# Hybrid decoder step on one core: the sample tokens' outer products as one fp32r matmul over 96 stacked rows, and their state products in four column groups

## The chip, the core and the metric

One Trainium2 chip (trn2), one of its cores. The metric is the device time of one execution in microseconds (us), the median of the runs shown; less is better. The core's engines are TensorE (PE; its weight loads are listed apart as PEld), VectorE (DVE), ScalarE (ACT), GpSimd (POOL) and SyncE (SP), which here only issues DMAs.

## The reference

One layer of a decoder for a prompt of 2048 tokens and, beside it, a batch of 8 sequences with 4 new tokens each (the 32 "sample" rows). Each token passes an HGRN2 recurrence and a sliding-window attention, which gates merge, and then an MLP with a squared ReLU. What the change touches is the recurrence of the sample rows, with four heads of 128 x 128 state for each of the 8 sequences:

```python
def step(S, inp):                       # one chunk; here the chunk is the 4 new tokens
    qc, lc, kc, vc = inp
    b = jnp.cumsum(lc, axis=-2)
    o_inter = jnp.einsum('bhcd,bhde->bhce', qc * jnp.exp(b), S)
    ...
    o_intra = jnp.einsum('bhts,bhse->bhte', attn, vc)
    bl = b[..., -1:, :]
    S_new = jnp.exp(bl[..., 0, :])[..., None] * S + jnp.einsum('bhsd,bhse->bhde', kc * jnp.exp(bl - b), vc)
    return S_new, o_inter + o_intra
```

`o_inter` is called the state products below, the second term of `S_new` the outer products. All arithmetic is float32.

## The kernel before

The prompt is worked in four blocks of 512 tokens, b0 to b3. The 32 sample rows (NS = 32) ride with block b3. Weights and activations of the large products are split into a high and a low part of type fp32r, and each product is three matmuls (high times high, high times low, low times high), lines 165 to 167, 264 to 266 and 1580 to 1582. The recurrence's own matmuls have float32 operands; such a matmul stands as two records in the trace, with two weight loads.

A scheduler sets the order on each engine when the kernel is built: the program text gives the dependences, and independent work of neighbouring stages is interleaved. Each engine then runs its list in that order and waits on semaphores. Buffers come from rings ("tags"); the next user of a ring's buffer waits until the last reader of it is done.

The part of block b3 that matters here, in order:

* Attention of the last prompt chunk: `pc_b3c` (masked probabilities, ring t4), `po_b3c` (values, line 1108), `ob_b` (its split, line 258).
* The recurrence's levels (`hgrn_levels`): at each of seven levels (two for the sample rows) DVE scales `W_b` (lines 776, 777), PE forms small blocks `lv_b3g` (prompt) and `lv_b3s` (sample) with line 771, four 32-row blocks of one PSUM bank side by side, and DVE copies them out under a mask (line 788). Matmuls of the gate columns, `ps_hgb`, are put between as filler.
* The chunk loop: `o_b3o`, `u_b3o`, `state`, one tail (`on_b3o`, transposes `oT_b3o`, line 1174) per chunk, with `ybb` matmuls (lines 165 to 167; `pb_b`, line 1258, takes their results on DVE) as filler.
* The sample part, lines 1209 to 1238, from 1387.7 us of the profile on. For each head h: SP loads the state `S0_h` (512 KB, shown as `S`, line 1221); PE multiplies `aS` by `vS` (one matmul, 32 rows, line 1222) and, for each of the 8 sequences b, a 128 x 32 column block of `qb` with `S0_h`'s block b (line 1224). All nine add up in the same 32 rows of PSUM, `o_smp`. `qb` holds a sequence's 4 query columns and zeros elsewhere, so the nine can share the rows. DVE spreads `vS` into `vb` (32 x 1024, row s only in its own sequence's block, line 1226) and scales `S0_h` (line 1230). Two matmuls `kn_smp` by `vb` (32 rows, 512 columns each, line 1233, `us`) give the outer products, DVE adds each to its half of `S0_h` (line 1234), and SP writes the state out (`out_new_s_sample`, line 1235).
* The sample tail: `hgrn_out` takes four sums of squares from `o_smp` on ACT (line 205), a power on POOL (line 200), and scales into `on_smp` on DVE (line 1164); `hgrn_tail` transposes it (`oT_smp`, line 1172). Then come the splits into `oa_b` and the `yab` matmuls.

`S0_h` and `vb_h` share the ring t4 of three buffers, so a load of the next state waits until the matmuls that read an older `vb` are done, and a `vb` may wait until a state has been written out. `kn_smp`, the `on_` tiles and others share the ring t2, also of three. SP issues state loads, state writes and weight loads (`r_ubb`, `r_uab`, line 138) in one list, so a waiting load holds up those behind it.

## Time and profile before

| | |
|---|---|
| median of 3 runs | 2823.07 us (2819.94 to 2825.53) |
| profiled execution | span 2810.0 us from the first to the last instruction; the 13.1 us to the median lie around it |
| PE busy | 2730.1 us (97% of the span) |
| DVE busy | 1791.2 us (64%) |
| ACT busy | 1110.0 us (40%) |
| POOL busy | 490.9 us (17%) |
| mean granted TensorE clock | 0.993 |

Times inside the program are counted from the span's start. A row of the timeline gives start, length, engine, line, operation, output and inputs, shape and count; in brackets stands the idle time of the engine before it and what ended that, where "issue" means that the profile shows nothing the engine waited for. The records of successive matmuls overlap, so what a matmul costs PE is read from start to start. Of a PE form such as 128*32 128x16, the first part is the weight block (contraction rows by columns) and the second the moving operand.

### The profile page before, as it was taken

Reading aid. Unit: us, or ns where it says so; the run is one execution under the profiler, and the core shown is the slowest. Engines: PE = TensorE matmul, PEld = TensorE weight load, DVE = VectorE, ACT = ScalarE, POOL = GpSimd, SP = SyncE. Lnnn points to the kernel's source line nnn. Section 1 sums busy time; section 2 is a strip of 40 time slices with the busy share of each in tenths; the row PEclk is TensorE's granted clock in tenths of the full one; section 3 lists DMA queues with packets and bytes.
Section 4 is the critical chain, followed back from the end, with each engine's and each line's share of the span. In section 5 each row is a group of like instructions: output and inputs, shape, how many; then the busy total and the mean of one; then the engine's idle time right before and its main releaser. Section 6 shows DMA issues by size and latency. Waiting matters only on the chain.

```text
span 2810.0 us, 50089 instructions
## 1 busy us (share of the span) xinstructions
PE 2730.1 (97%) x20053; PEld 2403.9 (86%) x20053; DVE 1791.2 (64%) x2905; ACT 1110.0 (40%) x2070; POOL 490.9 (17%) x782
## 2 busy tenths in 40 slices
PE   8999999999999999899999999999999999999998
PEld 7778888788899977677898888878888999999998
DVE  5675746746774385637667777765567777654556
ACT  4542445423344353335334333434344233343332
POOL 1100211002300102320231221220012343320001
PEclk9999999999999999999999999999999999999999
DMA  5237662377743424652365544796566444485553
GB/s 190 75 103 237 208 198 76 97 242 256 251 126 115 144 76 149 219 160 67 105 210 184 181 145 150 265 317 222 190 200 215 147 161 135 155 291 184 189 187 119
DMA packets 344481, 487.60 MB, mean 174 GB/s; under 512 B 23432, under 2 KB 220824, under 8 KB 344248
## 3 DMA queue, kind: packets, MB, share of 16 engines
q1 hardware_dynamic: 289112, 329.10, 37.5%
q0 software_dynamic: 42880, 140.22, 13.8%
q10 hardware_dynamic: 12256, 15.08, 1.5%
q8 instruction: 157, 2.57, 0.4%
q14 instruction: 76, 0.62, 0.1%
HBM read 353.64 MB, written 130.68 MB: 172 GB/s over the span
## 4 chain that ended last, share of the span: by engine, by line
PE 78%; DMA 6%; DVE 6%; issue 5%; ACT 2%; POOL 2%; SPq 0%; POOLq 0%; DVEq 0%; ACTq 0%
PE f L1581 6%; PE f L1582 6%; PE f L1580 6%; PE fB_f L264 4%; PE fB_f L266 3%; PE fB_f L265 3%; PE fD_f L264 2%; PE fD_f L266 2%; PE fD_f L265 2%; PE ps_hfb L684 2%; PE fB_z L264 1%; PE fB_z L266 1%; PE fB_z L265 1%; PE wob L1390 1%; PE gab L166 1%
## 5 line engine op out<-in xcount | busy, mean ns | idle before, releaser
L1582 PE MATMUL f<-f2S,lw2T 128*128 128x264 f32 (+1 forms) x576 | 184.4, 320 | 2.0 <-DVE lw2T L152 2.0
L1580 PE MATMUL f<-f2S,hw2T 128*128 128x264 f32 (+1 forms) x576 | 184.5, 320 | 1.6 <-ACT hw2T L151 1.6
L1581 PE MATMUL f<-f2S,hw2T 128*128 128x264 f32 (+1 forms) x576 | 184.0, 319 | 0.0
L264 PE MATMUL fB_f<-S,w1T_f 128*128 128x264 f32 (+1 forms) x384 | 123.2, 322 | 3.1 <-ACT c_f L327 2.2
L152 DVE TENSOR_TENSOR lw2T<-lw2T,hw2T 128x1024 fp32r<-128x1024 f32 x64 | 78.2, 1224 | 69.7 <-ACT hw2T L151 68.8
L265 PE MATMUL fB_f<-S,w1T_f 128*128 128x264 f32 (+1 forms) x384 | 122.5, 319 | 0.0
L1580 PE MATMUL f<-f2A,h_w2B 128*128 128x264 f32 (+1 forms) x384 | 122.4, 319 | 0.0
L1581 PE MATMUL f<-f2A,h_w2B 128*128 128x264 f32 (+1 forms) x384 | 122.3, 319 | 0.0
L1582 PE MATMUL f<-f2A,l_w2B 128*128 128x264 f32 (+1 forms) x384 | 122.3, 318 | 0.0
L266 PE MATMUL fB_f<-S,w1T_f 128*128 128x264 f32 (+1 forms) x384 | 122.0, 320 | 0.0
L151 ACT CAST hw2T<-lw2T 128x1024 fp32r<-128x1024 f32 x64 | 67.2, 1051 | 137.2 <-DMA lw2T<-w_T 137.2
L1582 PEld LDWEIGHTS f<-f2S,lw2T 128*128 128x128 f32 x576 | 108.4, 188 | 10.4 <-DVE lw2T L152 2.9
L1580 PEld LDWEIGHTS f<-f2S,hw2T 128*128 128x128 f32 x576 | 108.8, 189 | 9.9 <-ACT hw2T L151 2.4
L1388 PE MATMUL wob<-m_b,h_wob 128*128 128x512 f32 (+2 forms) x320 | 113.1, 353 | 3.2 <-ACT h_wob L257 3.2
L1390 PE MATMUL wob<-m_b,l_wob 128*128 128x512 f32 (+2 forms) x320 | 112.4, 353 | 3.0 <-DVE l_wob L258 2.8
L1581 PEld LDWEIGHTS f<-f2S,hw2T 128*128 128x128 f32 x576 | 108.8, 189 | 7.6
L1389 PE MATMUL wob<-m_b,h_wob 128*128 128x512 f32 (+2 forms) x320 | 112.5, 352 | 0.0
L152 DVE TENSOR_TENSOR f2S<-f2S 128x1024 fp32r<-128x1024 f32 (+1 forms) x64 | 78.9, 1240 | 41.3 <-ACT f2S L151 40.9
L257 ACT CAST w1T_f<-w1r_f 128x512 fp32r<-128x512 f32 x128 | 77.1, 619 | 69.7 <-DVE w1r_f L300 29.7
L258 DVE TENSOR_TENSOR w1T_f<-w1r_f,w1T_f 128x512 fp32r<-128x512 f32 x128 | 87.4, 688 | 26.0 <-ACT w1T_f L257 25.7
L1507 POOL DMA_DIRECT2D u_A<-c_f x106 | 57.4, 541 | 236.1 <-DVE c_f L1491 225.1
L1507 POOL DMA_DIRECT2D u_S<-s_f x144 | 77.7, 541 | 109.0 <-DVE s_f L1502 92.4
(845 smaller groups left out, 9256.8 us busy)
## 6 DMA issues: line engine op xcount, KB each, us to landing
w1r_f<-w_ff SPq DMA_DIRECT2D x64, 512.0 KB
lw2T<-w_T SPq DMA_DIRECT2D x64, 512.0 KB
rw2B<-w_ff SPq DMA_DIRECT2D x48, 512.0 KB
f2S<-u_S SPq DMA_DIRECT2D x32, 528.0 KB
ws<-w_ff SPq DMA_DIRECT2D x32, 512.0 KB
r_wob<-w_o SPq DMA_DIRECT2D x32, 512.0 KB
f2S<-u_S SPq DMA_DIRECT2D x32, 512.0 KB
u_S<-s_f POOLq DMA_DIRECT2D x96, 132.0 KB, 2.3
```

What stands on the lines that cost most here:

```text
L152: pin(nc.vector.tensor_tensor(lo, F(lo), F(hi), ALU.subtract), on)
L258: pin(nc.vector.tensor_tensor(dl, src, F(dh), ALU.subtract), on)
L264: nc.tensor.matmul(ps, wh, ah, start=(first and k == 0), stop=False, skip_group_check=not first)
L265: nc.tensor.matmul(ps, wh, al, start=False, stop=False, skip_group_check=not first)
L266: nc.tensor.matmul(ps, wl, ah, start=False, stop=(last and k == 3), skip_group_check=not first)
L1388: nc.tensor.matmul(p, wh, ah, start=(k == 0), stop=False)
L1389: nc.tensor.matmul(p, wh, al, start=False, stop=False)
L1390: nc.tensor.matmul(p, wl, ah, start=False, stop=(k == KD - 1))
L1507: nc.gpsimd.dma_start(us[o][u.n // 4][u.n % 4 * P:(u.n % 4 + 1) * P, u.t0:u.t0 + u.ln], y_)
L1580: nc.tensor.matmul(ps, wh, ah, start=first, stop=False, skip_group_check=cont)
L1581: nc.tensor.matmul(ps, wh, al, start=False, stop=False, skip_group_check=cont)
L1582: nc.tensor.matmul(ps, wl, ah, start=False, stop=lastk, skip_group_check=cont)
```

## The change

Four things change in the sample part.

1. The outer products. `kn3` holds 96 rows: the high part (fp32r) of the keys, their low part, and the high part again; `v3` holds high, high and low part of `vS`. One fp32r matmul over the 96 rows then gives the three products of a split pair. `vb` is spread from `v3`, 96 x 1024, and the mask `m_b` gets 96 rows. New instructions, once for all heads: four casts of 32 x 512 on ACT (one of them takes the place of the copy of `kn_smp`), two subtractions of 32 x 512 on DVE.
2. The state products. Sequence b's matmul writes the rows 32 (b mod 4) onward, so that four 32-row groups of the PSUM bank collect two sequences each. The `aS` by `vS` matmul comes last and adds to group 0.
3. At the end the four groups are added: one copy of 32 x 512 on ACT and three additions of 32 x 512 on DVE into `os`, and `hgrn_out` reads `os` instead of `o_smp`.
4. `kn3` and `v3` lie in the ring t2 and stay there over all heads.

```diff
-            kn = k_natural(kS, 0, NS, "smp")
+            kn3, v3 = (wk.tile([P, 512], F32R, tag="t2", bufs=3, name=n) for n in ("kn3", "v3"))
+            kps = k_turn(kS, 0, NS, "smp")
+            nc.scalar.copy(kn3[0:NS], kps[0:NS])
+            tt(kn3[NS:2 * NS], kps[0:NS], F(kn3[0:NS]), ALU.subtract)
+            nc.scalar.copy(kn3[2 * NS:3 * NS], F(kn3[0:NS]))
+            nc.scalar.copy(v3[0:NS], vS)
+            nc.scalar.copy(v3[NS:2 * NS], F(v3[0:NS]))
+            tt(v3[2 * NS:3 * NS], vS, F(v3[0:NS]), ALU.subtract)
...
-                nc.tensor.matmul(ops[0:NS, h * P:(h + 1) * P], aS[0:NS, h, :], vS[:, h * P:(h + 1) * P], start=True, stop=False)
                 for b in range(DB):
-                    nc.tensor.matmul(ops[0:NS, h * P:(h + 1) * P], qb[:, h, b * NS:(b + 1) * NS], S03[:, b, :], start=False, stop=(b == DB - 1))
-                vb = t4(f"vb_{h}")
+                    nc.tensor.matmul(ops[b % 4 * NS:(b % 4 + 1) * NS, h * P:(h + 1) * P], qb[:, h, b * NS:(b + 1) * NS], S03[:, b, :], start=(b < 4), stop=(b >= 4 and b % 4 > 0))
+                nc.tensor.matmul(ops[0:NS, h * P:(h + 1) * P], aS[0:NS, h, :], vS[:, h * P:(h + 1) * P], start=False, stop=True)
+                vb = t4(f"vb_{h}", F32R)
                 nc.vector.tensor_tensor(
-                    vb[0:NS].rearrange("p (b e) -> p b e", b=DB),
...
+                    vb[0:3 * NS].rearrange("p (b e) -> p b e", b=DB),
...
-                    nc.tensor.matmul(ups, kn[0:NS, h * P:(h + 1) * P], vb[0:NS, half * 512:(half + 1) * 512], start=True, stop=True)
+                    nc.tensor.matmul(ups, kn3[0:3 * NS, h * P:(h + 1) * P], vb[0:3 * NS, half * 512:(half + 1) * 512], start=True, stop=True)
...
-            on = hgrn_out(ops, NS, "smp")
+            os_ = t2("os")
+            nc.scalar.copy(os_[0:NS], ops[NS:2 * NS])
+            for o in (2, 3, 0):
+                tt(os_[0:NS], ops[o * NS:(o + 1) * NS], os_[0:NS], ALU.add)
+            on = hgrn_out(os_, NS, "smp")
```

The scheduler also moves work, since the first `vb` now needs `v3`. The numbers behind the names below tell buffers apart; lines after 1176 have moved by 4 to 15 in the new file (1221 is 1232, 1235 is 1246, 1258 is 1273).

SP's list around the first two state loads, before (`r_ubb` are weights for `ybb`, loaded in two halves; `r_uab` those for `yab`):

```order
L1221 DMA S_0_13841<-state_hgrn 128x8x128
L1221 DMA S_1_13862<-state_hgrn 128x8x128
L138 DMA r_ubb_14086<-w_up_b 64x4x256 x2
L138 DMA r_ubb_14149<-w_up_b 64x4x256 x2
L138 DMA r_uab_14231<-w_up_a 128x4x256
L1210 DMA out_new_s_prompt<-state 128x4x128
L1235 DMA out_new_s_sample<-S_0_13841 128x8x128
L1221 DMA S_2_13883<-state_hgrn 128x8x128
```

and now:

```order
L1232 DMA S_0_13847<-state_hgrn 128x8x128
L138 DMA r_ubb_14097<-w_up_b 64x4x256 x2
L138 DMA r_ubb_14160<-w_up_b 64x4x256 x2
L138 DMA r_uab_14242<-w_up_a 128x4x256
L1214 DMA out_new_s_prompt<-state 128x4x128
L1232 DMA S_1_13868<-state_hgrn 128x8x128
L1246 DMA out_new_s_sample<-S_0_13847 128x8x128
L1232 DMA S_2_13889<-state_hgrn 128x8x128
```

The second state's load has moved behind four weight loads and the write of the prompt's state.

DVE's list at the start of the levels, before:

```order
L1099 TENSOR_TENSOR pc_b3c_1_12836<-pT_b3c_1_12831,pc_b3c_1_12836 128x512
L1226 TENSOR_TENSOR vb_13852<-vS,cf 32x1024
L258 TENSOR_TENSOR ob_b_11900<-po_b3c_12855,ob_b_11900 128x4x128
L776 TENSOR_TENSOR W_b_11568<-W_b_11568,W_b_11569 128x4x128
L777 TENSOR_TENSOR W_b_11568<-W_b_11568,W_b_11569 128x4x128
```

and now:

```order
L1099 TENSOR_TENSOR pc_b3c_1_12836<-pT_b3c_1_12831,pc_b3c_1_12836 128x512
L258 TENSOR_TENSOR l_ubb_14034<-r_ubb_14030,h_ubb_14033 128x1024
L258 TENSOR_TENSOR ob_b_11900<-po_b3c_12855,ob_b_11900 128x4x128
L776 TENSOR_TENSOR W_b_11568<-W_b_11568,W_b_11569 128x4x128
L777 TENSOR_TENSOR W_b_11568<-W_b_11568,W_b_11569 128x4x128
```

The first `vb` has left this place, and `l_ubb`, the low part of a weight, stands there; before, it stood after the second level's copies (line 258 at 1332.64 us of the profile).

PE's list at the first two heads, before (`us_0_13855` and `us_1_13858` are the first head's outer products, `us_0_13876` and `us_1_13879` the second's; `ybb` rows are filler):

```order
L1224 MATMUL o_smp<-S_0_13841,qb 32x128 x8
L1233 MATMUL us_0_13855<-vb_13852,kn_smp 128x512
L1233 MATMUL us_1_13858<-vb_13852,kn_smp 128x512
L1222 MATMUL o_smp<-vS,W_b_11569 32x128
L1224 MATMUL o_smp<-S_1_13862,qb 32x128 x8
L1222 MATMUL o_smp<-vS,W_b_11569 32x128
L1233 MATMUL us_0_13876<-vb_13873,kn_smp 128x512
L1233 MATMUL us_1_13879<-vb_13873,kn_smp 128x512
L1172 MATMUL oT_b3o_13939<-ident,on_b3o_13818 128x128 x4
```

No filler stands among the two heads' products, and the prompt's last transposes (`oT_b3o`) come behind them. Now, on the same engine, from the first head's state products on:

```order
L1234 MATMUL o_smp<-S_0_13847,qb 32x128 x8
L1235 MATMUL o_smp<-vS,W_b_11569 32x128
L167 MATMUL ybb_288_14051<-ob_b_11900,l_ubb_14034 128x256
L165 MATMUL ybb_288_14051<-ob_b_11900,h_ubb_14033 128x256
L166 MATMUL ybb_288_14051<-ob_b_11900,h_ubb_14033 128x256
L167 MATMUL ybb_288_14051<-ob_b_11900,l_ubb_14034 128x256
L1172 MATMUL oT_b3o_13950<-ident,on_b3o_13818 128x128 x4
```

The transposes and filler have come ahead of the first `us`. Twelve more `ybb` matmuls follow; then PE's list goes on:

```order
L167 MATMUL ybb_0_14067<-ob_b_11900,l_ubb_14034 128x288
L1244 MATMUL us_0_13861<-vb_13858,kn_13827 128x512
L1244 MATMUL us_1_13864<-vb_13858,kn_13827 128x512
L1234 MATMUL o_smp<-S_1_13868,qb 32x128 x8
L1235 MATMUL o_smp<-vS,W_b_11569 32x128
L1244 MATMUL us_0_13882<-vb_13879,kn_13827 128x512
L1244 MATMUL us_1_13885<-vb_13879,kn_13827 128x512
L165 MATMUL ybb_288_14118<-ob_b_11900,h_ubb_14100 128x256
```

Between the first head's state products and its `us` there now stand 16 `ybb` matmuls and the four transposes, where nothing stood; after the second head's `us` come 12 `ybb`, then the third head's state products and `us`, then 24 `ybb`.

More of the change, by code (lines that the diff above doesn't have):

```diff
@@ L1174, in hgrn_tail, with k_turn @@
             nc.vector.tensor_tensor(go, tp.rearrange("p (h t) -> p h t", h=HH)[:, :, 0:nr], go, ALU.mult)
-        def k_natural(kx, k0, nr, name):
+        def k_turn(kx, k0, nr, name):
             tp = tp_ps("kn_" + name)
@@ L1179, in k_natural @@
                 nc.tensor.transpose(tp[0:nr, h * P:(h + 1) * P], kx[:, h, k0:k0 + nr], ident)
+            return tp
+        def k_natural(kx, k0, nr, name):
+            tp = k_turn(kx, k0, nr, name)
             kn = t2("kn_" + name)
@@ L1221, in tile_hybrid_step @@
                 nc.sync.dma_start(S03, s0[0].rearrange("b h d e -> d h b e")[:, h])
[L1222 removed]
                 for b in range(DB):
[L1224 to L1225 removed]
+                    nc.tensor.matmul(ops[b % 4 * NS:(b % 4 + 1) * NS, h * P:(h + 1) * P], qb[:, h, b * NS:(b + 1) * NS], S03[:, b, :], start=(b < 4), stop=(b >= 4 and b % 4 > 0))
+                nc.tensor.matmul(ops[0:NS, h * P:(h + 1) * P], aS[0:NS, h, :], vS[:, h * P:(h + 1) * P], start=False, stop=True)
+                vb = t4(f"vb_{h}", F32R)
                 nc.vector.tensor_tensor(
[L1227 to L1229 removed]
+                    vb[0:3 * NS].rearrange("p (b e) -> p b e", b=DB),
+                    F(v3)[0:3 * NS, h * P:(h + 1) * P].unsqueeze(1).broadcast_to([3 * NS, DB, P]),
+                    m_b[0:3 * NS].unsqueeze(2).broadcast_to([3 * NS, DB, P]), ALU.mult)
                 nc.vector.tensor_tensor(S03, S03, gl[:, h, :].unsqueeze(2).broadcast_to([P, DB, P]), ALU.mult)
@@ L1680, in _constants @@
     cf[:, 0:128] = i[:, None] <= i[None, :]
-    cf[0:NS, 128:136] = np.arange(NS)[:, None] // DS == np.arange(DB)[None, :]
+    cf[0:3 * NS, 128:136] = np.arange(3 * NS)[:, None] % NS // DS == np.arange(DB)[None, :]
     cf[:, 136:140] = i[:, None] // DS % G == np.arange(G)[None, :]
```

2 lines of the change are left out of this document (removed).

## The prediction

> **What bounds the kernel now.** I read the page's busy times, then its chain, then the groups and the timeline of the sample part.
>
> ```profile
> PE 2730.1 (97%) x20053; PEld 2403.9 (86%) x20053; DVE 1791.2 (64%) x2905; ACT 1110.0 (40%) x2070; POOL 490.9 (17%) x782
> PE 78%; DMA 6%; DVE 6%; issue 5%; ACT 2%; POOL 2%; SPq 0%; POOLq 0%; DVEq 0%; ACTq 0%
> ```
>
> PE works 97% of the span and is 78% of the chain that ends last, so PE work taken away counts in full where PE does not start to wait for something else. Whether it does is the question, and it is read in the stage itself (start and length of each row, then the idle time ahead):
>
> ```profile
> 1387.71 0.40 PE L1222 MATMUL o_smp<-vS,W_b 32*32 32x128 f32 x2
> 1388.04 1.94 PE L1224 MATMUL o_smp<-S,qb 128*32 128x128 f32 x16
> 1389.90 1.98 PE L1233 MATMUL us<-vb,kn_smp 32*128 32x512 f32 x4
> 1391.81 0.40 PE L1222 MATMUL o_smp<-vS,W_b 32*32 32x128 f32 x2
> ...
> 1400.79 1.91 PE L1224 MATMUL o_smp<-S,qb 128*32 128x128 f32 x16 [0.45 <-DMA S<-state_hgrn]
> 1404.63 1.93 PE L1224 MATMUL o_smp<-S,qb 128*32 128x128 f32 x16
> 1406.50 1.98 PE L1233 MATMUL us<-vb,kn_smp 32*128 32x512 f32 x4
> 1408.41 0.39 PE L167 MATMUL ybb<-ob_b,l_ubb 128*128 128x256 f32 x1
> ```
>
> Before, PE hardly waits here (0.45 us for the third state). A head's state products take 1389.90 - 1388.04 = 1.86 us, its outer products 1391.81 - 1389.90 = 1.91 us.
>
> **The PE work removed.** Two rows price the new forms, one fp32r matmul of 512 columns and column groups:
>
> ```profile
> 1254.89 0.39 PE L191 MATMUL ps_hib<-h_hib,hT_b 128*128 128x512 f32 x1
> 1255.12 0.40 PE L192 MATMUL ps_hib<-l_hib,hT_b 128*128 128x512 f32 x1
> 1325.65 1.94 PE L1108 MATMUL po_b3c<-pc_b3c,qkv_b 128*64 128x512 f32 x8
> ```
>
> An fp32r matmul of 512 columns starts 0.23 us after the one ahead, so the two `us` cost 0.46 instead of 1.91 us. Line 1108 writes two column groups: its 8 records of 512 columns take 1.94 us, as long as the 4 records of `us` in one group, so groups that lie apart run at once. With four groups, 16 records in 1.86 us become four rounds, 0.47 us. Per head that takes away 1.45 + 1.39 = 2.84 us, over four heads 11.4. This is an upper end: the pauses between `o_smp` and other forms lie in the 1.86 and stay; I count about 10.3. The lower end, groups that don't overlap at all, would leave 1.86 us per head and take away 5.8.
>
> **The sample stage, walked.** The first `us` now needs `v3`, whose low part DVE must subtract, and `kn3`. DVE's rows before, with one of ACT and two of PE as prices:
>
> ```profile
> 1388.90 0.69 DVE L1164 TENSOR_TENSOR on_b3o<-o_b3o,ors_b3o 128x512 f32<-128x512 f32 x1 [1.43 <-POOL ors_b3o L200]
> 1389.51 0.68 DVE L1174 TENSOR_TENSOR W_b<-oT_b3o,W_b 128x512 f32<-128x512 f32 x1
> 1390.11 1.22 DVE L1230 TENSOR_TENSOR S<-S,SV_b 128x1024 f32<-128x1024 f32 x1
> 1391.43 1.28 DVE L1234 TENSOR_TENSOR S<-S,us 128x512 f32<-128x512 f32 x2
> 1392.63 1.21 DVE L1226 TENSOR_TENSOR vb<-vS,cf 32x1024 f32<-32x1024 f32 x1
> ...
> 1398.70 0.40 DVE L1258 SCALAR_TENSOR_TENSOR pb_b<-pb_b,ybb 128x256 f32<-128x256 f32 x1
> ...
> 1387.22 0.58 ACT L1181 COPY kn_smp<-kn_smp 32x512 f32<-32x512 f32 x1
> ...
> 1397.21 0.30 PE L165 MATMUL ybb<-ob_b,h_ubb 128*128 128x288 f32 x1
> 1397.35 0.29 PE L166 MATMUL ybb<-ob_b,h_ubb 128*128 128x288 f32 x1
> ```
>
> In the new order DVE does `on_b3o` at 1388.90, line 1174, the subtractions for `kn3` and `v3` (0.61 each, as the step from 1388.90 to 1389.51), the scaling of the first state (1.2) and then the first `vb`, until about 1393.7. ACT's four casts (0.58 each, as the copy of `kn_smp`) lie beside `on_b3o` and line 1174. PE starts as before. It does the state products, the `aS` product and four `ybb` until 1389.2, waits 0.4 for `on_b3o`, does the transposes and 12 `ybb` (0.13 each, the step from 1397.21 to 1397.35) until 1391.65, and waits 2.05 for `vb`. The first `us` are done at 1394.15, the second state products at 1395.3. The second `vb` stands behind DVE's two additions to the first state (0.6 each) and its own 1.2: PE waits until 1396.65, 1.35 us. The next `ybb` needs a bank whose reader on DVE (`pb_b`, line 1258, 0.40) stands behind another scaling: 1.05 us until 1398.15. Twelve `ybb` end at 1399.6.
>
> Next come the state loads, which wait on SP for PE to be done with an older `vb`:
>
> ```profile
> 1396.35 0.38 SPq L1221 DMA_DIRECT2D S<-state_hgrn  x1
> 1397.07 0.37 SPq L1235 DMA_DIRECT2D out_new_s_sample<-S  x1
> 1400.37 0.38 SPq L1221 DMA_DIRECT2D S<-state_hgrn  x1
> ```
>
> By the two rows of `o_smp` at 1400.79 and 1404.63 above, a load issued at 1396.35 is used 4.44 us later and one at 1400.37 4.26 later; I take 4.35. The third state's load now waits for the second head's last `us` and goes at about 1397.3 (1396.35 before), so its state products start at 1401.65 after 2.05 us of waiting. The fourth's waits for the third head's `us`, which stand behind those products (before they stood ahead of them): 1403.2 instead of 1400.37, landed at 1407.55. The 24 `ybb` in between end at 1406.25 and PE waits 1.3. The last `us` ends at 1408.85; before it ended at 1408.41.
>
> Behind each waiting load on SP stand only the writes of states that are not read again here and later weight loads. New idle time is 0.4 + 2.05 + 1.35 + 1.05 + 2.05 + 1.3 = 8.2 us, and the work is smaller. In sum: up to the last `us` 52 `ybb` matmuls have run where 24 had. The 28, at 0.125 us between the wide and the narrow ones, are 3.5 us of work done earlier; less the 0.44 us of the later end and about 0.4 for the bank that the following `ybb` waits for, the stage gains 2.7 us. Bounds: 10.3 if all idle time vanished, and nothing if each load takes 1.3 us longer, since both loads stand in the path.
>
> The longer tail is costed at nothing: one copy on ACT (0.58) and three additions (0.61 each) delay `on_smp` by about 2.4 us, but `oT_smp` now stands behind some 60 `ybb` more than before, 7.5 us of PE work. With that cover gone it would cost 2.4 us.
>
> **The levels stage.** The first `vb` leaves DVE's list ahead of `ob_b`, and the second state's load leaves SP's list ahead of `r_ubb`. Both meet PE here:
>
> ```profile
> 1327.52 1.15 PE L771 MATMUL lv_b3g<-W_b 128*32 128x16 f32 x110
> 1331.08 0.40 PE L771 MATMUL lv_b3s<-W_b 128*32 128x16 f32 x8 [2.42 <-issue]
> 1332.59 1.39 PE L771 MATMUL lv_b3g<-W_b 128*32 128x16 f32 x125 [1.11 <-DVE W_b L777]
> 1336.09 0.29 PE L771 MATMUL lv_b3g<-W_b 128*32 128x16 f32 x3 [2.11 <-issue]
> ...
> 1327.62 1.21 DVE L1226 TENSOR_TENSOR vb<-vS,cf 32x1024 f32<-32x1024 f32 x1 [1.71 <-PE po_b3c L1108]
> 1328.76 0.67 DVE L258 TENSOR_TENSOR ob_b<-po_b3c,ob_b 128x512 fp32r<-128x512 f32 x1
> ...
> 1330.16:1333.57 3.41, 1.38 (x118) 1.34 (x122) 3.41 (x9) 0.95 (x4) 0.00 (x0) 1.00 1.02 220
> 1333.57:1336.98 3.41, 1.30 (x42) 1.18 (x32) 2.39 (x5) 1.66 (x3) 0.00 (x0) 0.50 0.02 5
> 1336.98:1340.39 3.41, 3.41 (x20) 3.09 (x20) 1.57 (x7) 0.00 (x0) 0.00 (x0) 0.50 0.02 5
> ...
> 1327.66 0.59 ACT L257 CAST ob_b<-po_b3c 128x512 fp32r<-128x512 f32 x1 [3.87 <-PE po_b3c L1108]
> ...
> q1 hardware_dynamic: 1570, 1.04, 60.6%
> q8 instruction: 1, 0.02, 3.7%
> ```
>
> Of the three windows the columns are length, busy PE, PEld, DVE, ACT and POOL, granted clock, DMA share and GB/s. The q1 row is all that the queues moved from 1326 to 1333.4: 1.04 MB, two parts of equal size, the second state and `r_ubb`. The q8 row is from 1333.4 to 1335.5: one packet of instructions, right after that traffic. PE's stall of 2.11 us that waits for nothing visible ends just after it, and I read it as PE waiting for its next instructions, held up by the 1.04 MB. Without the state's 0.5 MB the packet comes earlier and that stall goes. What is late next is DVE's chain of scaling and copying, at most 0.7 us behind: -1.4. The granted clock is 0.50 in the two windows after PE was busy only 1.38 of 3.41 us; in the second PE is fully busy, which at full clock would save half of it, 1.7, and in the first about 0.1. I count half, 0.9, since with two stalls of 2.42 and 1.11 left the clock may fall all the same. Together -2.3. Bounds: 0, and 2.11 + 1.8 + 0.46 (`ob_b` no longer behind `vb`, but behind ACT's cast, which ends at 1328.25: some 1328.30 instead of 1328.76) = 4.4.
>
> By the Trainium skill ("Runtime: NRT & Kernel Launch", section Instruction fetch mechanics) the sequencer fetches the next 16 KiB block of instructions by a DMA queue of its own while it runs the present one, and crossing a block is mostly hidden. By that rule the 2.11 us would be no fetch and the levels would give nothing; the packet's place behind the traffic speaks for a fetch that was not hidden.
>
> **Sum.** -2.7 - 2.3 = -5.0: the span goes from 2810.0 to 2805.0. The profiled execution has 13.1 us around it in the median of 2823.07, so I predict 2818.0. A measurement here tells about 0.2%, 5.6 us, from no change; the forecast lies just inside it.
>
> **Rivals.**
>
> A. PE stays the bound: `vb` and the loads come in time, because DVE gets ahead of PE. Then most of the 10.3 to 11.4 us counts: 2811.7 to 2815. For it speaks the 97%; against it that the first `vb` is behind five DVE operations and two loads of 4.35 us are started by PE itself. Chance 0.25.
>
> B. The levels give nothing, because the 2.11 us stays or the wait for DVE takes its place; only the sample stage's 2.7 remains: 2820.4. For it speaks that "issue" names no cause and that DVE is busy all 3.41 us of the window before. Chance 0.25. The skill's rule on fetches, above, would lead here.
>
> C. Slower: the new idle time of 8.2 us within some 21 halves the clock, as 1.38 busy of 3.41 us did above. A window at 0.50 in which PE would work fully costs 1.7 us. With the levels giving nothing, two windows (3.4) against 2.7 give 2823.8; three give 2825.5, and the sign turns at 1.6 windows. For it speaks that from 1395.1 to 1398.5 of the walk PE works only some 1.0 us. Against it: no other stretch of the walk has less than 1.3, and the stretch behind it has 2.05 us of waiting for the third state, which takes up a slower PE. The Trainium skill ("TensorE: Matmul & The Clock Gate", Part 1) lets the clock drop after an idle window, which none of the walked gaps fills; the row above, where 1.38 us of work did not keep it up, is stricter than that. Chance 0.12.
>
> **Chances and range.** The forecast's own case, 2815.5 to 2820, gets 0.38, A 0.25, B 0.25 (2820 to 2823), C 0.12. The range 2811 to 2824 takes in A's end and C's beginning and leaves out about 0.1 to 0.2. Faster by over 0.2% is below 2817.4: all of A and half of the forecast's case, 0.44. Slower by over 0.2% is above 2828.7, five windows of 1.7, or three and loads of 6 us, which delay the path by 1.65 twice: half of C, 0.06. Within: 0.50.
>
> **What would show it.** In the new profile: `us` records half as many with starts 0.23 apart; eight `o_smp` matmuls in about 0.5 us; PE idle behind the first state products for `vb` and in front of the third and fourth for the DMA of `S`, 4.3 to 4.5 us behind their issues; the "issue" stall near 1334 gone, with the q8 packet earlier; no half clock there. The forecast is wrong if the 2.11 us shows up elsewhere, if the waits for `vb` are short, or if the clock falls in the sample stage.

## The result and the profile after

The changed kernel takes 2827.41 us (median of 22 runs, 2818.55 to 2833.06), the kernel before 2821.93 us in the same series (22 runs): ratio 1.0017, interval 1.0010 to 1.0024. On two more occasions the ratio was 1.0022 (1.0010 to 1.0034) and 1.0018 (1.0004 to 1.0032). The change makes the kernel about 5 us slower; 5 us faster was forecast, and the time lies above the range.

The busy times and the chain of the page hardly moved:

```profile
PE 2732.2 (97%) x20045; PEld 2407.1 (85%) x20045; DVE 1796.0 (64%) x2910; ACT 1113.3 (39%) x2074; POOL 490.1 (17%) x782
PE 78%; DMA 7%; DVE 6%; issue 5%; ACT 2%; POOL 2%; SPq 0%; POOLq 0%; DVEq 0%; ACTq 0%
```

PE's busy time even rose by 2.1 us although some 10 us of matmuls were taken away. PE's clock enters this number: a matmul at half clock counts nearly twice as long (below, 1.01 us for eight products in place of 0.57). PE's timeline of the sample part, rows with waits and the products:

```profile
1391.84 0.64 PE L1234 MATMUL o_smp<-S,qb 128*32 128x128 f32 x16
1392.41 0.40 PE L1235 MATMUL o_smp<-vS,W_b 32*32 32x128 f32 x2
...
1394.37 0.66 PE L1172 MATMUL oT_b3o<-ident,on_b3o 128*128 128x128 f32 x4 [0.89 <-DVE W_b L1174]
...
1398.18 0.74 PE L1244 MATMUL us<-vb,kn 96*128 96x512 f32 x2 [1.56 <-DVE vb L1237]
1398.84 0.64 PE L1234 MATMUL o_smp<-S,qb 128*32 128x128 f32 x16
1399.42 0.54 PE L1235 MATMUL o_smp<-vS,W_b 32*32 32x128 f32 x2
1401.18 1.22 PE L1244 MATMUL us<-vb,kn 96*128 96x512 f32 x2 [1.23 <-DVE vb L1237]
1402.65 0.58 PE L165 MATMUL ybb<-ob_b,h_ubb 128*128 128x256 f32 x1 [0.24 <-DVE pb_b L1273]
...
1406.58 1.08 PE L1234 MATMUL o_smp<-S,qb 128*32 128x128 f32 x16 [0.99 <-DMA S<-state_hgrn]
...
1414.90 0.64 PE L1234 MATMUL o_smp<-S,qb 128*32 128x128 f32 x16 [0.51 <-DMA S<-state_hgrn]
```

The matmuls cost about what was forecast: eight state products take 0.57 us (1391.84 to 1392.41) where they took 1.86, and the two `us` of a head 0.66 us (1398.18 to 1398.84) where they took 1.91. The waits come where they were forecast, in the forecast order, together 5.4 us in these rows. But the products of the third head take 1.01 us (1406.58 to 1407.59), not 0.57. The windows say why (length, busy PE, PEld, DVE, ACT, POOL, granted clock, DMA share, GB/s):

```profile
1396.09:1399.50 3.41, 1.85 (x23) 1.05 (x23) 3.41 (x5) 0.00 (x0) 0.00 (x0) 1.00 0.35 104
1399.50:1402.91 3.41, 1.94 (x5) 0.81 (x6) 3.41 (x5) 0.00 (x0) 0.00 (x0) 0.51 0.50 154
1402.91:1406.33 3.42, 2.67 (x12) 2.38 (x12) 2.81 (x5) 0.00 (x0) 0.00 (x0) 0.50 0.73 213
1406.33:1409.74 3.41, 3.16 (x23) 2.23 (x24) 1.99 (x4) 0.00 (x0) 0.44 (x1) 0.50 0.31 94
1409.74:1413.15 3.41, 3.41 (x17) 3.41 (x16) 2.17 (x3) 0.00 (x0) 0.34 (x1) 0.50 0.65 191
```

After a window in which PE worked 1.85 of 3.41 us come four windows at half clock. The other profiles of the changed kernel have four there too.

I cut block b3 into three stretches by PE's rows: the levels (first `lv_b3g` to the last), the chunk loop (first `o_b3o` to first `o_smp`) and the sample part with the `yab` matmuls behind it (first `o_smp` to last `yab`). Their ends in the changed kernel's profile are

```profile
1314.69 0.36 PE L771 MATMUL lv_b3g<-W_b 128*32 128x16 f32 x18
...
1366.57 1.99 PE L771 MATMUL lv_b3g<-W_b 128*32 128x64 f32 x64
1370.29 0.46 PE L1197 MATMUL o_b3o<-SV_b,W_b 128*128 128x128 f32 x2
...
1455.67 0.28 PE L167 MATMUL yab<-oa_b,l_uab 128*128 128x256 f32 x1
```

so the levels take 51.88 us, the chunk loop 21.55 and the sample part 63.83. For all kernels of this study (a column holds one number for each profile; the ratio is to the kernel before on the same chip):

| kernel | levels | chunk loop | sample part | time, ratio |
|---|---|---|---|---|
| before | 48.25, 48.55, 47.79, 48.16 | 19.70, 19.97, 21.32, 19.98 | 62.64, 62.51, 62.64, 62.61 | 1 |
| the change | 51.88, 52.19, 52.03 | 21.55, 21.30, 21.31 | 63.83, 63.87, 63.91 | 1.0017, 1.0022, 1.0018 |
| outer products alone | 52.45 | 21.29 | 63.60 | 1.0031 |
| column groups alone | 48.22 | 19.98 | 62.74 | 1.0009 |
| change, `v3` early | 48.08 | 21.32 | 60.87 | 1.0000 |
| before, z early | 51.89 | 21.86 | 62.70 | 1.0020 |
| change, z late | 46.79, 47.09 | 22.18, 22.10 | 63.84, 63.90 | 1.0006, 0.9999 |
| before, z late | 48.35, 48.34 | 23.39, 23.29 | 62.77, 62.80 | 0.9980, 0.9987 |
| change, useless work | 51.46 | 21.72 | 65.28 | 1.0024 |
| change, useless work, z late | 47.67 | 21.76 | 65.44 | 0.9995 |
| change, three repairs | 48.40 | 22.82 | 58.75 | 0.9993 |
| column groups alone, z late | 47.67 | 22.16 | 63.74 | 0.9982 |
| change, `v3` early, z late | 47.46 | 22.18 | 60.84 | 0.9978 |

The loss is in the levels (+3.8 us between the means), the sample part (+1.3) and the chunk loop (+1.1). The first is a stretch in which the change has no instruction of its own. The chunk loop's time goes by its windows at half clock: in all the profiles it is 19.7 to 20.0 us with none, 21.3 to 22.2 with one and 22.8 to 23.4 with two.

**What happens in the levels.** From 1346 to 1350 us the queues moved (packets, MB, share of 16 engines; before first, then the changed kernel; q0 carries POOL's loads of `z` into `pb_b`, q1 SP's loads of the weights `r_ubb`):

```profile
q1 hardware_dynamic: 441, 0.43, 44.0%
...
q0 software_dynamic: 281, 1.11, 81.3%
q1 hardware_dynamic: 30, 0.03, 2.8%
```

SP issues the weights at nearly the same time in both kernels (first two rows, before and changed). POOL is what differs (the next two rows are of the kernel before, the last two of the changed one):

```profile
1346.56 1.26 SPq L138 DMA_DIRECT2D r_ubb<-w_up_b  x2
1346.11 1.26 SPq L138 DMA_DIRECT2D r_ubb<-w_up_b  x2
...
1346.16 4.17 POOL L1217 COPY qb<-W_b 128x32 f32<-128x32 f32 x3 [20.59 <-DVE pb_b L1146]
1350.28 1.50 POOL L1147 DMA_DIRECT2D pb_b<-z  x2
...
1344.35 0.77 POOL L1228 COPY qb<-W_b 128x32 f32<-128x32 f32 x3 [19.98 <-DVE pb_b L1146]
1345.08 1.51 POOL L1147 DMA_DIRECT2D pb_b<-z  x2
```

Before, the loads of `z` stood behind three small copies that took 4.17 us beside a DVE without a gap, and went 3.7 us behind the weights (1350.28 against 1346.56). Now DVE is ahead of PE and has a gap, the copies take 0.77 us, and the loads of `z` go 1.0 us ahead of the weights (1345.08 against 1346.11). By the Trainium skill ("SBUF — State Buffer", section SBUF: two separate sides) a GpSimd operation and a VectorE operation with two SBUF inputs take turns on one pair of ports; 4.17 against 0.77 us agrees. The same engines in the kernel before (DVE without a gap; ACT without a wait; PE's block of 128 small matmuls and the short stall behind it):

```profile
1346.71 1.21 DVE L258 TENSOR_TENSOR l_ubb<-r_ubb,h_ubb 128x1024 fp32r<-128x1024 f32 x1
1352.28 1.05 ACT L257 CAST h_ubb<-r_ubb 128x1024 fp32r<-128x1024 f32 x1
1354.11 1.32 PE L771 MATMUL lv_b3g<-W_b 128*32 128x16 f32 x128
1357.60 0.40 PE L165 MATMUL ps_hgb<-hT_b,h_hgb 128*128 128x288 f32 x1 [0.78 <-issue]
```

and in the changed one (DVE's gap; ACT; PE's stall at the start of the levels, which the prediction was about; the block of 128 and the stall behind it):

```profile
1346.00 1.22 DVE L258 TENSOR_TENSOR l_ubb<-r_ubb,h_ubb 128x1024 fp32r<-128x1024 f32 x1 [0.95 <-PE ps_hgb L166]
...
1354.99 1.05 ACT L257 CAST h_ubb<-r_ubb 128x1024 fp32r<-128x1024 f32 x1 [3.13 <-DMA r_ubb<-w_up_b]
...
1334.71 0.29 PE L771 MATMUL lv_b3g<-W_b 128*32 128x16 f32 x3 [2.09 <-issue]
...
1353.59 1.32 PE L771 MATMUL lv_b3g<-W_b 128*32 128x16 f32 x128
1358.35 0.43 PE L165 MATMUL ps_hgb<-hT_b,h_hgb 128*128 128x288 f32 x1 [2.05 <-issue]
```

ACT waits 3.13 us for weights that were there before it asked in the old order, and the gates of the next level stand behind it. PE's stall "<-issue" behind the block of 128, 0.78 us before, is 2.05 us now. A window at half clock follows it (columns as above), which no profile of the kernel before has there:

```profile
1355.18:1358.59 3.41, 1.36 (x10) 1.13 (x9) 2.52 (x4) 1.51 (x3) 0.00 (x0) 1.00 0.66 229
1358.59:1362.00 3.41, 3.20 (x42) 2.54 (x43) 3.14 (x8) 2.75 (x7) 0.00 (x0) 0.50 0.04 8
```

From the start of that block to the last `lv_b3g` the kernel before takes 10.1 to 10.2 us in its four profiles and the changed kernel 13.0, 14.6 and 14.6. The longer stall, waits of 0.2 to 1.0 us for DVE's copies (line 788) and this window make it up.

### The profile page after: what moved, and what is told of

Same layout as the page of the kernel before. It is cut to its first block, busy times and chain, and to the rows that moved or that the text cites. A ratio compares the mean times of both kernels' runs of the same rounds, so it can differ in the third digit from the quotient of the medians.

```text
span 2820.9 us, 50080 instructions
## 1 busy us (share of the span) xinstructions
PE 2732.2 (97%) x20045; PEld 2407.1 (85%) x20045; DVE 1796.0 (64%) x2910; ACT 1113.3 (39%) x2074; POOL 490.1 (17%) x782
## 3 DMA queue, kind: packets, MB, share of 16 engines
q8 instruction: 157, 2.57, 0.4%
## 4 chain that ended last, share of the span: by engine, by line
PE 78%; DMA 7%; DVE 6%; issue 5%; ACT 2%; POOL 2%; SPq 0%; POOLq 0%; DVEq 0%; ACTq 0%
PE f L1597 6%; PE f L1596 6%; PE f L1595 6%; PE fB_f L264 4%; PE fB_f L266 4%; PE fB_f L265 3%; PE ps_hfb L684 2%; PE fD_f L264 2%; PE fD_f L266 2%; PE fD_f L265 2%; PE fB_z L264 1%; PE fB_z L266 1%; PE fB_z L265 1%; PE wob L1405 1%; DMA w1r_f<-w_ff 1%
```

## The experiments

The first four tell which part costs what.

The changed kernel again:

> The changed kernel once more, for a second profile of it and for times on the same chip as the other three. Theory (idle and clock): PE's new waits in the sample part, some 5.6 us in the first profile (0.89, 1.56, 1.23, 0.24, 0.99, 0.51 and shorter ones), halve its clock for three or four windows of 3.41 us behind them, in every run; the time is 4 to 7 us above the kernel before. Rival (chance): the windows run free, so the 13.7 us of half clock in the first profile were bad luck; a second profile shows at most one such window there, and the time is within 2 us of the kernel before. The 22 runs of the change fall into two groups near 2821 and 2829 us; if a bistable wait makes them, the two profiles differ by about 8 us in one place.

2822.53 us, ratio 1.0022. The second profile agrees with the first in all three stretches and has the four windows of half clock (1400.03 to 1413.68), so chance as an explanation falls. The waits for ACT's weights are there again (4.53 us). The two groups of times near 2821 and 2829 us stay unexplained: all three profiles of the change are of the faster one (2822.74, 2823.81 and 2821.91 us).

Outer products alone (the state products as before, the rest of the change kept):

```diff
-                for b in range(DB):
-                    nc.tensor.matmul(ops[b % 4 * NS:(b % 4 + 1) * NS, h * P:(h + 1) * P], ...
-                nc.tensor.matmul(ops[0:NS, ...], aS[0:NS, h, :], ..., start=False, stop=True)
+                nc.tensor.matmul(ops[0:NS, ...], aS[0:NS, h, :], ..., start=True, stop=False)
+                for b in range(DB):
+                    nc.tensor.matmul(ops[0:NS, ...], ..., start=False, stop=(b == DB - 1))
...
-            on = hgrn_out(os_, NS, "smp")
+            on = hgrn_out(ops, NS, "smp")
```

> Only the outer products are changed (96 rows, one fp32r matmul); the state products stay in one group, with the aS by vS product first. The long state products (1.86 us a head) fill some of the waits for vb. Theory (idle and clock): PE's idle time of the sample part falls from about 6 us to 2 to 4, the clock stays at 1.00 there or drops for one window; the time lies between the kernel before and the full change, +0 to +4 us against before. Rival (the late second state and first vb alone cost the time): as slow as the full change, +4 to +7.

2823.10 us, ratio 1.0031 (1.0019 to 1.0043): the rival's value. The levels are 52.45 us, so whatever lengthens them comes with the outer products, whose `vb` needs `v3`, and not with the column groups. The sample part has no half clock from 1378.5 to 1419.5, as the theory had it, yet is only 0.3 us shorter than in the full change: its state products take 1.9 us a head again.

Column groups alone (`kn`, `vb` and `us` as before):

> Only the state products are changed (four column groups, sums added at the end); kn and vb stay as before, and so do the places of the first vb and of the second state's load. Theory (idle and clock): nothing new waits on DVE ahead of the first us, so the 5.6 us of PE work are mostly a gain: -2 to -5 us against before, clock 1.00 in the sample part. Rival (the four groups with their longer tail, or the loads of the third and fourth state, cost the time): +0 to +4.

2818.44 us, ratio 1.0009 (1.0001 to 1.0018). The levels are those of before; the sample part is 62.74 us, so the 5.2 us of matmuls saved (four times 1.29) bring nothing. PE waits 0.67 and 0.96 us for `vb`, and two windows (1395.0 to 1401.9) run at half clock. The rival's +0 to +4 held.

The full change with `v3` made early:

```diff
+            v3 = wk.tile([P, 512], F32R, tag="v3s", bufs=1, name="v3")    # ahead of the levels
+            nc.scalar.copy(v3[0:NS], vS)
+            nc.scalar.copy(v3[NS:2 * NS], F(v3[0:NS]))
+            tt(v3[2 * NS:3 * NS], vS, F(v3[0:NS]), ALU.subtract)
```

> The full change, but v3 is made from vS before the recurrence's levels and lies in a buffer of its own. The first vb and the second state's load are then back at their old places, and the first two heads' state products and us stand together as in the kernel before. Theory (idle and clock): the waits of 0.89, 1.56 and 1.23 us go, what remains are the waits for the third and fourth state (about 1 to 2 us); no or one window of half clock in the sample part; -3 to -8 us against before, 8 to 12 faster than the full change. Rival (loads): PE then arrives earlier at the third state and waits 3 us and more there; the clock falls all the same, and the time is within 2 us of the full change.

2814.35 us, ratio 1.0000 (0.9988 to 1.0012). DVE's order at the start of the levels is that of before again, and the levels are 48.08 us. The sample part is 60.87 us, 1.7 under before; the waits for `vb` went, one of 2.76 us for a bank that DVE frees came, and three windows of half clock stayed. Faster than the full change, but not by the 8 to 12 us expected.

The next four test the collision in the levels and the clock in the sample part.

The change with the loads of `z` let go later (this moves block b2's loads as well):

```diff
-            if zs and rnd in (3, 5):
-                for j in (2 * rnd - 6, 2 * rnd - 4):
+            if zs and rnd in (5, 6):
+                for j in ((0, 2) if rnd == 5 else (4, 6)):
```

> The changed kernel with one thing else: the four loads of z into pb_b on POOL's queue (544 KB each) are let go two recurrence levels later, behind the issue of the weights r_ubb. Theory (collision): in both profiles of the change the first two of these loads go 5 us earlier than before, take the DMA engines from the weights, and ACT waits 3 to 5 us for them ahead of the gates that free PE's banks. With the loads late the stretch from the first lv_b3 to the last one falls from 52 us to 48 or less, the half clock at 1358 goes, and the kernel is 3 to 4 us faster than the change. Rival (the levels are slow because of DVE's new order or by the phase of the clock windows): the stretch stays at 51 us or more.

2821.52 us, ratio 1.0006 (0.9992 to 1.0019). The levels fall from 52.0 to 46.79 us. ACT finds the weights there, and PE's stall behind the block of 128 is gone, with the window at half clock behind it:

```profile
1354.54 1.06 ACT L257 CAST h_ubb<-r_ubb 128x1024 fp32r<-128x1024 f32 x1
...
1353.77 2.94 POOL L1147 DMA_DIRECT2D pb_b<-z  x4 [5.81 <-PE ps_hgb L167]
...
1356.12 1.32 PE L771 MATMUL lv_b3g<-W_b 128*32 128x16 f32 x128
1359.32 0.70 PE L771 MATMUL lv_b3g<-W_b 128*32 128x32 f32 x32 [0.22 <-DVE SV_b L788]
```

The kernel before with the harm alone (the four copies into `qb` on ACT, so that POOL has nothing ahead of the loads of `z`):

```diff
-                nc.gpsimd.tensor_copy(qb[:, h, :].rearrange("p (b x) -> p b x", x=36)[:, :, 0:DS], ...
+                nc.scalar.copy(qb[:, h, :].rearrange("p (b x) -> p b x", x=36)[:, :, 0:DS], ...
```

> The kernel before, with the four small copies into qb done by ACT instead of POOL and nothing of the change in it. POOL then has nothing ahead of the loads of z, which go about 4 us earlier, as in the changed kernel. Theory (collision): r_ubb comes late, ACT waits for it 2 to 5 us, the stretch of the levels grows from 48.2 to about 51 us, and the time by 2 to 4 us, with none of the change. Rival: the levels stay at 48 us, the time within 1 us of the kernel before.

2826.33 us, ratio 1.0020 (1.0005 to 1.0035). With none of the change in it, this kernel is as slow as the changed one, has its levels (51.89 us) and its waits:

```profile
1359.40 1.05 ACT L257 CAST h_ubb<-r_ubb 128x1024 fp32r<-128x1024 f32 x1 [3.75 <-DMA r_ubb<-w_up_b]
...
1361.49 0.40 PE L165 MATMUL ps_hgb<-hT_b,h_hgb 128*128 128x288 f32 x1 [1.39 <-issue]
1363.63 0.70 PE L771 MATMUL lv_b3g<-W_b 128*32 128x32 f32 x32 [1.61 <-DVE SV_b L788]
```

So the collision alone is enough for a slowdown of this size, and taking it away gives the levels back. It does not give the whole time back: with the same late loads the kernel before is faster than the change (below).

The change with useless work for PE:

```diff
+                    for _ in range(6 if half == 0 else 0):
+                        nc.tensor.matmul(ups, ob[:, 0, 0, 0:P], ob[:, 0, 1, 0:512], start=True, stop=True)
                     nc.tensor.matmul(ups, kn3[0:3 * NS, h * P:(h + 1) * P], ...
```

> The changed kernel with 24 useless matmuls of 512 columns, six into the bank of each head's first outer product ahead of it (0.22 us each, 5.3 us in all), so that PE works where it waited for vb and for the states. Theory (clock): the sample part keeps more of the full clock than the four windows at 0.50 of the change, the stretch from the first o_smp to the last ybb (39.8 us) grows by at most 2, though 5.3 us of work were added. Rival (the clock doesn't matter there): the waits that are left don't shrink by what was added, and the stretch grows by 3 us or more.

2825.93 us, ratio 1.0024 (1.0012 to 1.0036), as slow as the change without them. The sample part grows by 1.4 us (65.28 against 63.87) though 5.3 us of matmuls were added, and one window there runs at half clock in place of four:

```profile
1401.29:1404.70 3.41, 1.30 (x4) 0.79 (x5) 3.41 (x6) 0.00 (x0) 0.00 (x0) 1.00 0.00 0
1404.70:1408.11 3.41, 3.41 (x23) 1.86 (x22) 2.39 (x3) 0.00 (x0) 0.00 (x0) 0.50 0.55 158
1408.11:1411.53 3.42, 3.42 (x19) 2.84 (x18) 3.11 (x6) 0.00 (x0) 0.00 (x0) 1.00 0.35 93
```

The waits shrink by little (0.38, 1.97, 0.55, 1.15 and 1.11, 5.2 us in all), so of the 3.9 us that disappear most must be the clock: some 3 us for three windows.

The full change with three repairs (`v3` early and the loads of `z` late by the edits above, and `vb` spread on ACT):

```diff
-                nc.vector.tensor_tensor(
-                    vb[0:3 * NS].rearrange("p (b e) -> p b e", b=DB), ...
+                for b in range(DB):
+                    nc.scalar.mul(vb[0:3 * NS, b * P:(b + 1) * P], F(v3)[0:3 * NS, h * P:(h + 1) * P], m_b[0:3 * NS, b:b + 1])
```

> The full change with three repairs: v3 is made before the levels in a buffer of its own; vb is spread by eight scaled copies per head on ACT instead of one product on DVE (1.2 us each); the loads of z are let go two levels later. Theory: no new wait for vb or for r_ubb, waits for the third and fourth state of 1 to 3 us remain; 4 to 8 us faster than the kernel before. Rival (state loads and clock windows take it all): within 2 us of the kernel before.

2818.97 us, ratio 0.9993 (0.9981 to 1.0005). The sample part is the shortest of all, 58.75 us, 3.9 under before; levels 48.40, chunk loop 22.82 with two windows of half clock. The time is the rival's.

The next four ask what is left without the collision, and what the profile of before was worth.

> The kernel before once more, for a second profile. The profile on which the prediction rests had a span of 2810.0 us, 10 us under the median of 35 runs on this chip. Theory (lucky profile): its chunk loop (first o_b3o to first o_smp, 19.70 us) had no window of half clock by chance; a second profile shows one or two there and 21 to 22 us, with levels of 48 us and a sample part (first o_smp to last yab) of 62.7 us as before. Rival: the chunk loop takes 19.7 us again, and the 1.6 us more of the changed kernels there are an effect of the change.

2808.36 us in its one execution: chunk loop 19.97, levels 48.55, sample part 62.51. There is no half clock in its chunk loop either, so the theory of a lucky one falls for this profile; the third profile of this kernel, below, has one such window and 21.32 us.

The kernel before with the loads of `z` late (same edit as above):

> The kernel before with the loads of z let go two levels later, and nothing of the change. Theory (collision): before, the z loads came just behind the weights and cost little; the levels go from 48.2 to about 47, and the time is 0 to 2 us below the kernel before. Rival: the levels of the changed kernel with late loads (46.8 us) are short because of its other order, and here they stay at 48.

2813.46 us, ratio 0.9980 (0.9972 to 0.9989). Its levels stay at 48.35 us and its chunk loop is longer (23.39), so the gain does not lie in b3 by its profile. The levels are the rival's; a gain of 5 us neither side had. What lengthens the chunk loop is PE's next stall of this kind, at the blocks `lx_b3g`, with two windows at half clock; the kernel before first, then this run:

```profile
1369.27 0.60 PE L805 MATMUL lx_b3g<-W_b 128*32 128x1 f32 x50 [0.57 <-issue]
...
1368.44 0.91 PE L805 MATMUL lx_b3g<-W_b 128*32 128x1 f32 x50 [1.93 <-issue]
```

Six of the eight profiles with late loads show 1.65 to 1.93 us there, and the kernel before 0.57 to 0.84 in its four profiles. So the late loads seem to move a part of the collision to the next stage; this was not tried alone.

> The four column groups alone, with the loads of z let go two levels later. Theory: the levels take 46.5 to 48 us, the sample part 62 to 63 as in the run of the groups alone, since its waits for vb and half clock took the gain; 0 to 2 us below the kernel before. Rival: with the levels shorter DVE comes earlier, the waits for vb go, and the sample part falls under 61 us.

2813.14 us, ratio 0.9982 (0.9969 to 0.9996): levels 47.67, sample part 63.74. The column groups are worth nothing here either.

> The full change, v3 made before the levels in a buffer of its own, and the loads of z let go two levels later. Theory: levels 46.5 to 48 us, sample part 60 to 61.5 us, together 2 to 4 us below the kernel before and 7 to 9 below the change. Rival (the clock windows take what the waits leave): within 1 us of the kernel before.

2810.28 us, ratio 0.9978 (0.9966 to 0.9990): levels 47.46, sample part 60.84. It is the fastest kernel found, 0.2% under the kernel before, but not apart from the kernel before with the loads of `z` late.

Six more, since the size of the parts was open. Four stood side by side:

> The kernel before with late loads of z, again, beside the next three on one chip. Theory: as in the first run of it, 4 to 6 us below the kernel before; some executions of the kernel before then have the collision too, though neither of its profiles shows it. Rival: the first run was lucky, and it lies within 2 us of the kernel before.

> The change with late loads of z, again. Theory (two parts): against the run beside it without the change it is 1 to 4 us slower: this is what the waits and the half clock of the sample part cost more than the matmuls save, since nothing collides in either. Rival (the 7 us by which the first runs of the two differed are real): 6 us and more slower, which the sample part of the profiles, 1.2 us longer, would not explain.

> The change as it is, beside the run with late loads. Theory (collision): 3 to 5 us slower than that run, 4 to 7 slower than the kernel before. Rival: within 2 us of the run with late loads.

> The change with late loads of z and the 24 useless matmuls (5.3 us) of the earlier run. Theory (clock): one window of half clock in the sample part instead of four, so the time grows by less than 2 us over the run without the useless matmuls. Rival (the clock there costs nothing): it grows by 3 to 5 us.

The ratios are 0.9987 (0.9976 to 0.9998), 0.9999 (0.9988 to 1.0010), 1.0018 (1.0004 to 1.0032) and 0.9995 (0.9981 to 1.0008), the medians 2813.55, 2820.16, 2822.07 and 2817.38 us. The change as it is lies 0.0019 (5 us) above the one with late loads by the ratios, as the collision has it, and 1.9 us by the medians. With late loads in both, the change is still 0.0012 (3.4 us) above the kernel before by the ratios, and 6.6 us by the medians. The useless 5.3 us cost nothing that the times show: the fourth is not slower than the second, though its sample part, with one window at half clock (1397.6 to 1401.0) instead of four, is 1.5 us longer.

Two more executions of the kernel before, without edit, for the question whether it collides at times:

> A third profile of the kernel before. Two profiles of it lie 8 to 11 us under its median and show no collision, yet letting the z loads go late made it 4 to 5 us faster. Theory (some executions collide): if this execution is near the median (2819 us), POOL's copies into qb take under 1.1 us instead of 4.2, ACT waits 2 us or more for r_ubb, the levels take 51 us or more. Rival: an execution near the median shows levels of 48 us, and its time lies elsewhere.

> A fourth profile of the kernel before, with the same question: levels of 51 us and a wait of ACT for r_ubb in an execution near the median by the theory, 48 us and no wait by the rival.

2808.51 and 2818.76 us. The second is at the median, and its levels are 48.16 us, with POOL's copies at 4.19 us and no wait of ACT for the third `h_ubb`:

```profile
1350.81 4.19 POOL L1217 COPY qb<-W_b 128x32 f32<-128x32 f32 x3 [20.70 <-DVE pb_b L1146]
...
1356.98 1.05 ACT L257 CAST h_ubb<-r_ubb 128x1024 fp32r<-128x1024 f32 x1
```

The rival held: what makes this execution 10 us longer than the third lies ahead of b3 (its first gate matmul of b3, `ps_hib`, starts at 1242.3 us against 1233.2) and behind it, not in the collision.

## Why the prediction was wrong, point by point

* **The price of the matmuls** was nearly right: 0.57 us for eight state products (0.47 forecast, the pause before the next form left out), 0.66 us for the two `us` of a head at full clock (0.46 forecast). That saves 2.54 us a head, 10.2 in all, where 10.3 were counted on. Four column groups do run at once.
* **The walk of the sample part** named the right waits: 0.4 for `on_b3o` (0.89 measured, up to the end of line 1174, the next step of DVE), 2.05 and 1.35 for `vb` (1.56 and 1.23), 1.05 for the bank (0.24), 2.05 and 1.3 for the states (0.99 and 0.51). From the first state products to the end of the last `us` it had 20.8 us (1388.04 to 1408.85); measured are 24.3 (1391.84 to 1416.14, the start of the next row). The waits were 2.8 us shorter than forecast (5.4 against 8.2), so the work took 6.3 us longer. The clock is most of it: PE was busy 11.2 us in the four windows at 0.50 above, and at full clock about half of that, 5.6 us, would have done (an estimate). The step that failed is the weighing of rival C: "the stretch behind it has 2.05 us of waiting ... which takes up a slower PE". The clock did not come back after one window; it stayed at 0.50 for four, through the `ybb` matmuls that were to be the gain. So the term -2.7 measured +1.3 (63.87 against 62.60 between the means). With the clock at 1.00 in three of the four windows the sample part would have taken about 60.9 us (3 us less, an estimate from the run with useless work), 1.7 under before, where 2.7 were forecast.
* **The levels' -2.3** failed at its first step, "I read it as PE waiting for its next instructions, held up by the 1.04 MB". The stall is 2.09 us in the changed kernel, with half the traffic gone: nothing moved from 1329.0 to 1332.3, and the packet came after that, 1.4 us behind the start of PE's block of 125 matmuls (1330.93). The rows of the queues from 1332.3 to 1334:

```profile
q8 instruction: 1, 0.02, 3.2%
```

  I read it as a fetch, since in every profile PE goes on 2 to 3 us behind the packet, but not as one held up by loads: nothing was ahead of it. That it was asked for late is argued, not shown. So the stall stayed, as rival B had it, whose 2820.4 had nothing lost on top. By the Trainium skill ("Runtime: NRT & Kernel Launch", section Instruction fetch mechanics) such a fetch is mostly hidden; here 125 matmuls are run in 1.7 us and it is not.
* **What was missing** is the largest term: the levels grew by 3.8 us. The prediction asked what the moved load and the moved `vb` would free, and stopped at "what is late next is DVE's chain". An engine that is early lets a third one, POOL, start transfers early. The two loads' order on two queues was never in the sum. The mechanism sought at the first stall does exist at the other one: there the packet of instructions came 1.1 us behind the start of the block of 128 matmuls in the kernel before (1355.21) and 2.2 us in the changed kernel (1355.82); `z` filled the queues in both then (96% and 106% of 16 engines from 1355.0 to 1355.5). With early loads in the kernel before it came 1.6 us behind the start, and with late loads in the change ahead of the block.
* **The base.** The prediction took 13.1 us as what lies around the span. In the profiled executions since, the time is the span plus 1.7 to 2.1 us (2822.74 for 2820.9). So the profile was of an execution of about 2811.8 us, faster than any of the 22 runs of the kernel before. Since the sum is a difference this moved nothing, but it says how far one execution may lie from the median.

Sum by the profiles: +3.8 in the levels, +1.1 in the chunk loop and +1.3 in the sample part, 6.2 us; measured are 4.8 (0.0017) to 6.2 (0.0022). The prediction had nothing for the chunk loop. The +1.1 is one window at half clock there. It is not shown to come from the collision: the third profile of the kernel before (21.32) and the change with `v3` early (21.32) have the window without a collision, so for this term it may be chance how the windows fall.

**What stays open.** Late loads speed up the kernel before by 0.13 to 0.20%, though from the first `lv_b3g` to the last `yab` its profiles get longer (138.2 and 138.1 us, against 134.3 to 135.5); the edit also moves loads in block b2, and nothing was run for that alone. With late loads in both, the change is 3.4 and 7.3 us slower (0.0012 and 0.0026). Its sample part is 1.1 us longer, but its levels and its chunk loop are shorter, and from the first `lv_b3g` to the last `yab` it takes 136.5 and 136.8 us, 1.5 less than the kernel before with late loads. So this loss doesn't lie in b3 by the profiles, and where it lies was not found. The mean granted clock of those runs, 0.9893 against 0.9913 in the last series, fits the four more windows at half clock that the profile of the change has; only two of them are in b3. That DVE's gap is why POOL's copies run fast was read from the rows, not tried alone.

## What to carry to other kernels

Ask of a change off the critical path not only what it frees, but which transfer an engine that is now early will start, and which load that is waited for stands behind it on the DMA engines. Work taken from PE in a stage where another engine or a load sets the pace may cost more than nothing: waits of 1 to 2 us in a row can take the clock away from the filler that was to be the gain. Compare stretches of the program between the same rows in several profiles; the whole time of one execution, 2808 to 2819 us for one and the same kernel here, cannot carry a term of 3 us.

## What the runs showed of the hardware that was not expected

* A granted clock of 0.50 came after windows in which PE was busy 1.85 of 3.41 us (the change), 1.64 (its second profile), 2.45 (the column groups alone) and 2.78 (the same with late loads), and it stayed for up to four windows in which PE was busy 1.9 to 3.4 us. By the Trainium skill ("TensorE: Matmul & The Clock Gate", Part 1) an idle window brings it down; here none was idle.
* PE's busy share alone does not tell whether the clock falls. At one place of the chunk loop PE was busy 2.57 us of a window in the third and in the second profile of the kernel before; behind it the clock was 0.50 in the one and 1.00 in the other (two windows of each):

```profile
1362.20:1365.61 3.41, 2.57 (x124) 2.22 (x114) 1.12 (x4) 0.35 (x2) 0.00 (x0) 1.00 0.24 93
1365.61:1369.02 3.41, 3.41 (x18) 3.41 (x17) 0.00 (x0) 1.00 (x5) 0.00 (x0) 0.50 0.02 5
...
1361.98:1365.39 3.41, 2.57 (x78) 2.23 (x79) 0.63 (x3) 0.35 (x2) 0.00 (x0) 1.00 0.13 42
1365.39:1368.80 3.41, 3.38 (x30) 3.17 (x29) 0.48 (x2) 2.33 (x10) 0.47 (x2) 1.00 0.00 0
```

  The windows cut the same rows at different places: in the one 1.32 us of the busy time are matmuls of one column (line 805), in the other 0.90. What the clock goes by was not tried.
* Three POOL copies of 128 x 32 took 4.17 to 4.19 us beside a DVE without gaps (kernel before), and 0.77 to 1.00 us where DVE had one (the change).
* PE's instruction packets came up to 3.2 us behind the start of a block of 128 small matmuls where loads filled the queues, 1.1 us with the kernel before, and the stall behind it was 2.0 to 2.9 instead of 0.7 to 0.8 us.
